# A hybrid encoder on one core: every second weight unit of the mixers is split by transfers instead of by VectorE or GpSimd

## The chip, the core and the metric

The kernel runs on one core of one Trainium2 chip. The metric is the device time of one execution in microseconds. TensorE multiplies; ScalarE (ACT), VectorE (DVE) and GpSimd (POOL) do the elementwise work; SyncE (SP) issues the transfers. Work on one engine runs in the order in which it was queued there; engines wait for each other by semaphores.

## The reference

Two layers (DEPTH = 2) over 256 tokens of 1024 features, all in float32. Each layer is a feed-forward half step, a mixer with four branches, and another feed-forward half step:

```python
for l in range(DEPTH):
    x = x + 0.5 * swiglu_ffn(x, ffn1_norm[l], ffn1_wi[l], ffn1_wo[l])
    h = rmsnorm(x, mix_norm[l])
    (a_q, a_k, a_v, sc_u, c_qlat, c_kvlat, c_krope, lru_u, gate_lin) = jnp.split(
        h @ w_in[l], split_idx, axis=-1)
    o_a = gqa_mixer(...)        # 8 query heads, 2 key/value heads, rotary
    o_b = shortconv_mixer(...)  # width-3 convolution, gated
    o_c = mla_mixer(...)        # low-rank attention, 8 heads
    o_d = rglru_mixer(...)      # width-4 convolution, gated recurrences both ways
    branches = jnp.stack([o_a, o_b, o_c, o_d], axis=2)
    y = jnp.einsum('bsnc,ncd->bsnd', branches, w_branch[l])
    g = jax.nn.sigmoid(gate_lin.reshape(b, s, N_BRANCH, d))
    x = x + jnp.sum(g * y, axis=2) @ w_out[l]
    x = x + 0.5 * swiglu_ffn(x, ffn2_norm[l], ffn2_wi[l], ffn2_wo[l])
```

A feed-forward half step has matrices of 1024 x 5632 and 2816 x 1024. The mixer's `w_in` is 1024 x 8096, `w_branch` 4 x 512 x 1024, `w_out` 1024 x 1024; the low-rank up-projections and the recurrence's gates are small.

## The kernel before

**Products in three parts.** Every float32 operand is kept as a high and a low part, both in the type float32r, that sum to it. A product is three matmuls (`mm`, lines 208 to 212): high by high, high by low, low by high. Each weight piece of 128 rows by 128 columns (some are 336, 384 or 512 columns wide) meets all 256 tokens.

**The stream of weights.** The class `Weights` (line 66) streams all weights once, in the order of their use. That order is found by a first pass over the program with `Null` objects. `chunks_of` (line 134) groups the pieces into units of at most 1024 columns (`UNIT`; the first two are smaller), and units into transfers of at most 2048 columns (`MAXC`), except the first seven (`FIRST`), which hold one unit each and go to buffers of their own. `load` (line 82) issues one transfer on SP into a tile of `raw_pool` (three buffers of 2048 columns). `split` (line 100) makes a unit's parts:

```python
a = self.nc.scalar.copy(hi[:, :w], src)
self.n += 1
eng = self.nc.gpsimd if self.share and self.n % self.share == 0 else self.nc.vector
b = eng.tensor_tensor(lo[:, :w], src, hi[:, :w].bitcast(F32), op=ALU.subtract)
```

So ScalarE casts the unit to `hi` (line 110) and VectorE or GpSimd subtracts it from the raw weights to give `lo` (line 113). There are four buffers each for `hi` and `lo`. `next` (line 121) hands out pieces and calls `split` so that two units (`AHEAD`) are called for ahead of the one in use. `share` decides who subtracts: 0 is VectorE alone; from the mixer's first slot until `gate(3, 0)` it is 4, every fourth unit on GpSimd; from the slot of head 15 until the output projection it is 1, all on GpSimd.

**The start.** Lines 233 to 242 issue on SP four transfers of `x`, ten transfers of weights (`EARLY`) and then the identity, the parameters and the tables, in that order. The identity is used first in `scale_rows` (line 358).

**A mixer.** It begins with token-major products of the latents and of queries, keys and values. Then comes a list of slots (line 905): each has an attention head or none, some products to keep TensorE fed (input projections, gates, branch up-projections), and other work. The grouped-query heads (0 to 7) run beside the short convolution and the recurrence, the low-rank heads (8 to 15) beside the gates. Of the other work GpSimd has: the rotary swaps (line 311), powers for the norms, the recurrence's products over 1024 columns (lines 709 to 711, 722, 723), a product of the gelu (667), squares (803, 808) and the gated sums (880). A head takes VectorE's row maximum (448), the exponential on ScalarE (454), a scaling of the probabilities on VectorE (462), transposes on TensorE (469), their split (217, 218) and the value products on TensorE (966).

**Order.** The program is written with tile pools; a planner orders the instructions on each engine by their place in the program, their dependencies and its own estimate of durations, and gives out buffers. Only the instructions marked `keep_in_program_order` (the constants' transfers and the opening work) keep their place.

Of the kernel before, what the change touches and what calls it, by code (L numbers as in the profile page):

```python
# [17 lines left out]
T = 256  # L18
# [10 lines left out]
# columns of the combined input projection  # L29
# [11 lines left out]
# per-layer columns of the packed per-channel parameters  # L41
# [7 lines left out]
# per-layer columns of the packed row vectors, then the rotary tables  # L49
# [7 lines left out]
# the first transfers of weights hold one unit each; so many of them go ahead of the constants  # L57
FIRST = 7
EARLY = 10
# GQA heads between a head's scores and its use  # L60
LAG = 2
# opening work in order: operand pair of x's tile k (k), split of the next weights (-1), square of tile k (10 + k)
START = (0, -1, 1, 2, 3, -1, 4, 5, -1, 6, 7, -1, 10, 11, 12, -1, 13, 14, 15, 16, 17)


class Weights:
    """Streams the weights in the order of their use and hands out each piece as two float32r
    parts that sum to it. Without the packed array it only records that order."""

    AHEAD = 2  # L70

    def __init__(self, nc, flat=None, order=None, raw_pool=None, hi_pool=None, lo_pool=None):
# [5 lines left out]
        self.spare = None  # where the first transfers go  # L78
        self.share, self.n = 0, 0  # every share-th low part on GpSimd
        self.ci, self.off, self.loaded, self.ready, self.now = 0, 0, [], [], []  # L80

    def load(self):
        if self.recording:
            return
        units = self.chunks[self.ci]
# [7 lines left out]
        self.off += P * cols  # L93
        self.ci += 1
        at = 0
        for u in units:
            self.loaded.append((u, raw, at))
            at += sum(p[4] for p in u)

    def split(self):  # L100
        if self.recording:
            return ()
        if not self.loaded:
            self.load()
        u, raw, at = self.loaded.pop(0)
        w = sum(p[4] for p in u)
        hi = self.hi_pool.tile([P, UNIT], F32R, tag="hi", name="hi")
        lo = self.lo_pool.tile([P, UNIT], F32R, tag="lo", name="lo")
        src = raw[:, at : at + w]
        a = self.nc.scalar.copy(hi[:, :w], src)  # L110
        self.n += 1
        eng = self.nc.gpsimd if self.share and self.n % self.share == 0 else self.nc.vector
        b = eng.tensor_tensor(lo[:, :w], src, hi[:, :w].bitcast(F32), op=ALU.subtract)  # L113
        out, o = [], 0
        for p in u:
            out.append((p, hi[:, o : o + p[4]], lo[:, o : o + p[4]]))
            o += p[4]
        self.ready.append(out)
        return a, b

    def next(self, *piece):
# [3 lines left out]
        if not self.now:  # L125
            while len(self.ready) <= self.AHEAD and (self.loaded or self.ci < len(self.chunks)):
                self.split()
            self.now = self.ready.pop(0)
# [5 lines left out]
def chunks_of(order):  # L134
    """Pieces grouped into split units of at most UNIT columns, those into transfers of MAXC."""
# [20 lines left out]
class Null:  # L156
    """Stands for every object of a trace that only records the order of the weights."""
# [18 lines left out]
def hybrid_encoder(ctx: ExitStack, tc: tile.TileContext, xT, par, rows, ident_d, flat, out, order=None):  # L176
# [31 lines left out]
    def mm(out, lhs, rhs, start, stop):  # L208
        """out (+)= lhs.T @ rhs, each operand a (high, low) pair of float32r."""
# [4 lines left out]
    def split(hi, lo, src, scale=None):  # L214
        """hi + lo = src (times a per-partition or constant scale)."""
# [931 lines left out]
```

## Time and profile before

| what | value |
|---|---|
| median of 3 runs (lowest to highest) | 1417.77 us (1417.46 to 1418.06) |
| profiled execution, span from first to last instruction | 1416.7 us |
| busy share: TensorE, VectorE, ScalarE, GpSimd | 97%, 71%, 53%, 17% |
| transfers | 240.81 MB, 170 GB/s on average |
| granted TensorE clock, mean | 0.990 |

The profiled execution's own time is shown as its span; the three runs have no profile. The four feed-forward half steps and the two mixers follow each other: the first mixer runs from about 200 to 505 us of the span, the second from about 900 to 1210 us. In the profile, L12 is line 12 of the kernel. A tile is shown by its program name (`hi<-raw`: reads raw, writes hi). "PEclk" is the clock that TensorE was granted, 1.00 being the full 2.4 GHz. A matmul's listed duration overlaps that of its neighbours, so the rate of matmuls is read from counts or from start times.

### The profile page before, as it was taken

Reading aid. Unit: us, or ns where it says so; the run is one execution under the profiler, and the core shown is the slowest. Engines: PE = TensorE matmul, PEld = TensorE weight load, DVE = VectorE, ACT = ScalarE, POOL = GpSimd, SP = SyncE. Lnnn points to the kernel's source line nnn. Section 1 sums busy time; section 2 is a strip of 40 time slices with the busy share of each in tenths; the row PEclk is TensorE's granted clock in tenths of the full one; section 3 lists DMA queues with packets and bytes.
Section 4 is the critical chain, followed back from the end, with each engine's and each line's share of the span. In section 5 each row is a group of like instructions: output and inputs, shape, how many; then the busy total and the mean of one; then the engine's idle time right before and its main releaser. Section 6 shows DMA issues by size and latency. Waiting matters only on the chain.

```text
span 1416.7 us, 26507 instructions
## 1 busy us (share of the span) xinstructions
PE 1377.8 (97%) x11184; PEld 1364.5 (96%) x11184; DVE 999.4 (71%) x1334; ACT 746.0 (53%) x1104; POOL 247.0 (17%) x199
## 2 busy tenths in 40 slices
PE   8999999997999999999999999999989999999999
PEld 8999999897899999999999999999889999999999
DVE  6666558989877676666566665599899777666653
ACT  6444447584556555444444444566745564554432
POOL 3200004329610400000000000032456104000000
PEclk9999999999999999999999999999999999999999
DMA  7555545433454355555555555444325534555552
GB/s 280 184 187 191 183 152 202 149 120 129 155 179 149 120 180 188 193 184 179 183 180 194 188 179 180 163 176 165 118 108 183 197 127 149 179 179 181 186 206 76
DMA packets 35831, 240.81 MB, mean 170 GB/s; under 512 B 3968, under 2 KB 5376, under 8 KB 9472
## 3 DMA queue, kind: packets, MB, share of 16 engines
q1 hardware_dynamic: 35712, 239.12, 47.6%
q8 instruction: 87, 1.43, 0.4%
q14 instruction: 32, 0.26, 0.1%
HBM read 238.06 MB, written 1.05 MB: 169 GB/s over the span
## 4 chain that ended last, share of the span: by engine, by line
PE 88%; DVE 5%; issue 2%; POOL 2%; ACT 1%; DMA 0%; SPq 0%; DVEq 0%; POOLq 0%; ACTq 0%
PE pg L211 6%; PE pu L211 6%; PE pg L212 6%; PE pg L210 6%; PE pu L212 6%; PE pu L210 6%; PE po L211 6%; PE po L210 6%; PE po L212 6%; PE pgt L210 4%; PE pgt L211 3%; PE pgt L212 3%; PE pa L211 2%; PE pa L212 2%; PE pa L210 2%
## 5 line engine op out<-in xcount | busy, mean ns | idle before, releaser
L110 ACT CAST hi<-raw 128x1024 fp32r<-128x1024 f32 (+4 forms) x459 | 474.2, 1035 | 500.5 <-PE po L211 117.0
L113 DVE TENSOR_TENSOR lo<-raw,hi 128x1024 fp32r<-128x1024 f32 (+4 forms) x428 | 539.5, 1261 | 276.1 <-ACT hi L110 274.5
L210 PE MATMUL pg<-xh,hi 128*128 128x256 f32 x704 | 199.0, 283 | 6.1 <-ACT hi L110 6.1
L211 PE MATMUL pg<-xl,hi 128*128 128x256 f32 x704 | 199.5, 283 | 0.0
L212 PE MATMUL pg<-xh,lo 128*128 128x256 f32 x704 | 199.2, 283 | 0.0
L211 PE MATMUL pu<-xl,hi 128*128 128x256 f32 x704 | 198.8, 282 | 0.0
L210 PE MATMUL pu<-xh,hi 128*128 128x256 f32 x704 | 198.4, 282 | 0.0
L212 PE MATMUL pu<-xh,lo 128*128 128x256 f32 x704 | 198.3, 282 | 0.0
L211 PE MATMUL po<-hl,hi 128*128 128x256 f32 x704 | 198.0, 281 | 0.0
L212 PE MATMUL po<-hh,lo 128*128 128x256 f32 x704 | 197.7, 281 | 0.0
L210 PE MATMUL po<-hh,hi 128*128 128x256 f32 x704 | 197.7, 281 | 0.0
L210 PE MATMUL pgt<-xnh,hi 128*128 128x256 f32 x512 | 146.4, 286 | 0.0
L212 PE MATMUL pgt<-xnh,lo 128*128 128x256 f32 x512 | 145.0, 283 | 0.7 <-DVE lo L113 0.7
L211 PE MATMUL pgt<-xnl,hi 128*128 128x256 f32 x512 | 145.5, 284 | 0.0
L210 PEld LDWEIGHTS pg<-xh,hi 128*128 128x128 f32 x704 | 133.8, 190 | 6.4 <-ACT hi L110 6.4
L212 PEld LDWEIGHTS pg<-xh,lo 128*128 128x128 f32 x704 | 133.8, 190 | 0.2 <-DVE lo L113 0.2
L211 PEld LDWEIGHTS pg<-xl,hi 128*128 128x128 f32 x704 | 133.8, 190 | 0.0
L212 PEld LDWEIGHTS pu<-xh,lo 128*128 128x128 f32 x704 | 133.1, 189 | 0.2 <-DVE lo L113 0.2
L211 PEld LDWEIGHTS pu<-xl,hi 128*128 128x128 f32 x704 | 133.2, 189 | 0.0
L210 PEld LDWEIGHTS pu<-xh,hi 128*128 128x128 f32 x704 | 133.0, 189 | 0.0
L211 PEld LDWEIGHTS po<-hl,hi 128*128 128x128 f32 x704 | 132.7, 188 | 0.0
L212 PEld LDWEIGHTS po<-hh,lo 128*128 128x128 f32 x704 | 132.6, 188 | 0.0
(301 smaller groups left out, 3052.7 us busy)
## 6 DMA issues: line engine op xcount, KB each, us to landing
raw<-weights SPq DMA_DIRECT2D x205, 1024.0 KB, 4.8
raw<-weights SPq DMA_DIRECT2D x9, 768.0 KB, 4.3
raw<-weights SPq DMA_DIRECT2D x4, 896.0 KB, 4.6
raw<-weights SPq DMA_DIRECT2D x3, 1008.0 KB, 4.7
raw<-weights SPq DMA_DIRECT2D x5, 512.0 KB, 8.0
out<-xg SPq DMA_DIRECT2D x8, 128.0 KB, 2.1
raw<-weights SPq DMA_DIRECT2D x1, 1016.0 KB, 4.8
raw<-weights SPq DMA_DIRECT2D x1, 968.0 KB, 4.6
```

What stands on the lines that cost most here:

```text
L110: a = self.nc.scalar.copy(hi[:, :w], src)
L113: b = eng.tensor_tensor(lo[:, :w], src, hi[:, :w].bitcast(F32), op=ALU.subtract)
L210: TE.matmul(out, lhs[0], rhs[0], start=start, stop=False)
L211: TE.matmul(out, lhs[0], rhs[1], start=False, stop=False)
L212: TE.matmul(out, lhs[1], rhs[0], start=False, stop=stop)
```

## The change

Units with an odd number whose pieces all belong to the mixers (`w_in`, `lru`, `qup`, `kvup`, `wb`, `wout`) are "queued". Such a unit is never loaded raw. GpSimd issues a transfer from the weights in memory to `hi`, which casts to float32r on its way; ScalarE writes the negative of `hi` into `lo`; GpSimd issues a second transfer of the same weights that adds to `lo`. All other units are split as before, always with VectorE; `share` is gone. `prepare` calls a queued unit up to four units ahead of the one in use (`LEAD`), others two ahead as before. `raw_pool` has two buffers instead of three, `hi_pool` and `lo_pool` five instead of four. A transfer holds one unit alone where it or its neighbour is queued. Comments are blanked too, which keeps the line numbers of unchanged places near their old ones.

```diff
+QUEUED = ("w_in", "lru", "qup", "kvup", "wb", "wout")
+
+def queued(i, unit):
+    return i % 2 == 1 and all(p[0] in QUEUED for p in unit)
...
     AHEAD = 2
+    LEAD = 4
...
     def load(self):
         if self.recording:
             return
+        while len(self.chunks[self.ci]) == 1 and queued(self.unit_of(self.ci), self.chunks[self.ci][0]):
+            self.skip()
...
+    def pair(self):
+        hi = self.hi_pool.tile([P, UNIT], F32R, tag="hi", name="hi")
+        lo = self.lo_pool.tile([P, UNIT], F32R, tag="lo", name="lo")
+        return hi, lo
...
         a = self.nc.scalar.copy(hi[:, :w], src)
-        self.n += 1
-        eng = self.nc.gpsimd if self.share and self.n % self.share == 0 else self.nc.vector
-        b = eng.tensor_tensor(lo[:, :w], src, hi[:, :w].bitcast(F32), op=ALU.subtract)
...
+        b = self.nc.vector.tensor_tensor(lo[:, :w], src, hi[:, :w].bitcast(F32), op=ALU.subtract)
         return a, b
+
+    def queue(self, n):
+        _, src, w, _ = self.units[n]
+        self.made[n] = hi, lo = self.pair()
+        self.nc.gpsimd.dma_start(hi[:, :w], src)
+        self.nc.scalar.activation(lo[:, :w], hi[:, :w].bitcast(F32), AF.Copy, scale=-1.0)
+        self.nc.gpsimd.dma_start(lo[:, :w], src, accum_op=ALU.add)
+
+    def prepare(self):
+        for n in range(self.taken, min(self.taken + self.LEAD + 1, len(self.units))):
+            if n in self.made:
+                continue
+            if self.units[n][3]:
+                self.queue(n)
+            elif n <= self.taken + self.AHEAD:
+                while n not in self.made:
+                    self.split()
...
-        if cur and (n + w > MAXC or i <= FIRST):
+        if cur and (n + w > MAXC or i <= FIRST or queued(i, u) or queued(i - 1, units[i - 1])):
...
-    raw_pool = ctx.enter_context(tc.tile_pool(name="raw_pool", bufs=3))
-    hi_pool = ctx.enter_context(tc.tile_pool(name="hi_pool", bufs=4))
-    lo_pool = ctx.enter_context(tc.tile_pool(name="lo_pool", bufs=4))
+    raw_pool = ctx.enter_context(tc.tile_pool(name="raw_pool", bufs=2))
+    hi_pool = ctx.enter_context(tc.tile_pool(name="hi_pool", bufs=5))
+    lo_pool = ctx.enter_context(tc.tile_pool(name="lo_pool", bufs=5))
...
-        def share(n):
-            return lambda: setattr(W, "share", n)
```

## Rows read from the trace of the kernel before

**Rows 1.** us from:to, length; busy us (count) of PE, PEld, DVE, ACT, POOL; PEclk, DMA share, GB/s.

```profile
200.00:240.00 40.00, 40.00 (x269) 40.00 (x268) 28.27 (x55) 27.11 (x53) 8.13 (x16) 1.00 0.56 195
240.00:300.00 60.00, 57.83 (x468) 55.58 (x466) 57.08 (x84) 36.49 (x64) 25.11 (x27) 1.00 0.40 142
300.00:362.00 62.00, 51.13 (x364) 48.65 (x364) 55.22 (x66) 37.24 (x64) 40.16 (x14) 0.92 0.36 127
...
400.00:480.00 80.00, 79.89 (x680) 79.68 (x679) 57.16 (x91) 48.18 (x89) 7.55 (x5) 1.00 0.41 146
480.00:505.00 25.00, 22.64 (x177) 22.23 (x176) 16.54 (x29) 10.21 (x18) 14.75 (x7) 0.93 0.46 163
...
940.00:1000.00 60.00, 59.44 (x483) 57.51 (x482) 57.02 (x87) 38.02 (x69) 20.78 (x16) 1.00 0.42 145
1000.00:1060.00 60.00, 51.13 (x371) 49.00 (x370) 51.40 (x66) 36.33 (x63) 31.65 (x13) 0.94 0.32 112
...
1180.00:1210.00 30.00, 27.01 (x203) 26.60 (x203) 22.16 (x35) 12.33 (x21) 14.94 (x7) 0.89 0.34 117
60.00:180.00 120.00, 120.00 (x1011) 120.00 (x1011) 74.16 (x86) 55.79 (x66) 0.00 (x0) 1.00 0.53 187
```

**Rows 2.** TensorE in order of time, 318 to 362 us: start, duration, instruction, wait.

```profile
328.51 0.58 PE L966 MATMUL pov<-pl,vg 128*128 128x256 f32 x1 [4.53 <-DVE pl L218]
...
329.54 0.41 PE L210 MATMUL pgt<-xnh,hi 128*128 128x256 f32 x1
329.75 0.41 PE L211 MATMUL pgt<-xnl,hi 128*128 128x256 f32 x1
```

**Rows 3.** VectorE's and GpSimd's groups, 240 to 380 us: busy us, mean ns | idle.

```profile
L113 DVE TENSOR_TENSOR lo<-raw,hi 128x1024 fp32r<-128x1024 f32 x26 | 35.2, 1354 | 8.6 <-ACT hi L110 8.4
L462 DVE TENSOR_SCALAR pe<-pe,sm 128x256 f32<-128x256 f32 x16 | 15.8, 1031 | 0.2
...
L113 DVE TENSOR_TENSOR lo<-raw,hi 128x768 fp32r<-128x768 f32 x3 | 6.0, 2009 | 0.0
...
L113 POOL TENSOR_TENSOR lo<-raw,hi 128x1024 fp32r<-128x1024 f32 x8 | 20.1, 2512 | 34.9 <-ACT hi L110 34.9
L113 POOL TENSOR_TENSOR lo<-raw,hi 128x768 fp32r<-128x768 f32 x1 | 6.6, 6557 | 0.0
```

**Rows 4.** VectorE in order of time: two pairs of the softmax scaling.

```profile
317.24 4.69 DVE L462 TENSOR_SCALAR pe<-pe,sm 128x256 f32<-128x256 f32 x2
...
476.56 0.62 DVE L462 TENSOR_SCALAR pe<-pe,sm 128x256 f32<-128x256 f32 x2
```

**Rows 5.** The weight split's groups: the page's casts, then 60 to 180 us.

```profile
L110 ACT CAST hi<-raw 128x1024 fp32r<-128x1024 f32 (+4 forms) x459 | 474.2, 1035 | 500.5 <-PE po L211 117.0
...
L113 DVE TENSOR_TENSOR lo<-raw,hi 128x1024 fp32r<-128x1024 f32 x43 | 52.5, 1222 | 29.2 <-ACT hi L110 29.2
L110 ACT CAST hi<-raw 128x1024 fp32r<-128x1024 f32 x42 | 44.0, 1048 | 60.2 <-PE po L211 20.3 <-PE pg L211 19.9 <-PE pu L211 17.8
```

**Rows 6.** Transfers by size: count, KB each, median us from issue to landing.

```profile
raw<-weights SPq DMA_DIRECT2D x205, 1024.0 KB, 4.8
...
raw<-weights SPq DMA_DIRECT2D x5, 512.0 KB, 8.0
...
raw<-weights SPq DMA_DIRECT2D x1, 744.0 KB, 4.2
...
ident<-ident SPq DMA_DIRECT2D x1, 64.0 KB, 13.9
```

**Rows 7.** The opening in order of time: SP's issues, TensorE's use of the identity.

```profile
10.13 0.33 SPq L242 DMA_DIRECT2D ident<-ident  x1
...
22.44 35.71 SPq L92 DMA_DIRECT2D raw<-weights  x7
...
26.73 0.61 PE L358 MATMUL pb<-ident,rt 128*128 128x128 f32 x4
```

**Rows 8.** GpSimd in order of time: two of the recurrence's products.

```profile
327.40 5.95 POOL L711 TENSOR_TENSOR thi<-thi,thr 128x1024 f32<-128x1024 f32 x2
```

More of the change, by code (lines that the diff above doesn't have):

```diff
@@ L78, in __init__ @@
         self.spare = None
-        self.share, self.n = 0, 0
         self.ci, self.off, self.loaded, self.ready, self.now = 0, 0, [], [], []
+        self.units, at = [], 0
+        for c in self.chunks:
+            cols = sum(p[4] for u in c for p in u)
+            o = 0
+            for u in c:
+                w = sum(p[4] for p in u)
+                src = flat[at : at + P * cols].rearrange("(p c) -> p c", p=P)[:, o : o + w]
+                self.units.append((u, src, w, queued(len(self.units), u)))
+                o += w
+            at += P * cols
+        self.made, self.taken = {}, 0
     def load(self):
@@ L92, in load, with unit_of, skip @@
         self.nc.sync.dma_start(raw[:, :cols], src)
-        self.off += P * cols
+        at, first = 0, self.unit_of(self.ci)
+        self.skip()
+        for i, u in enumerate(units):
+            self.loaded.append((first + i, raw, at))
+            at += sum(p[4] for p in u)
+    def unit_of(self, ci):
+        return sum(len(c) for c in self.chunks[:ci])
+    def skip(self):
+        self.off += P * sum(p[4] for u in self.chunks[self.ci] for p in u)
         self.ci += 1
[L95 to L98, printed above, removed]
+    def pair(self):
+        hi = self.hi_pool.tile([P, UNIT], F32R, tag="hi", name="hi")
+        lo = self.lo_pool.tile([P, UNIT], F32R, tag="lo", name="lo")
+        return hi, lo
     def split(self):
@@ L104, in split @@
             self.load()
[L105 to L108, printed above, removed]
+        n, raw, at = self.loaded.pop(0)
+        w = self.units[n][2]
+        self.made[n] = hi, lo = self.pair()
         src = raw[:, at : at + w]
         a = self.nc.scalar.copy(hi[:, :w], src)
-        self.n += 1
-        eng = self.nc.gpsimd if self.share and self.n % self.share == 0 else self.nc.vector
-        b = eng.tensor_tensor(lo[:, :w], src, hi[:, :w].bitcast(F32), op=ALU.subtract)
[L114 to L118, printed above, removed]
-        return a, b
+        b = self.nc.vector.tensor_tensor(lo[:, :w], src, hi[:, :w].bitcast(F32), op=ALU.subtract)
+        return a, b
+    def queue(self, n):
+        _, src, w, _ = self.units[n]
+        self.made[n] = hi, lo = self.pair()
+        self.nc.gpsimd.dma_start(hi[:, :w], src)
[10 more added lines that the diff above has]
+                    self.split()
     def next(self, *piece):
@@ L125, in next @@
         if not self.now:
-            while len(self.ready) <= self.AHEAD and (self.loaded or self.ci < len(self.chunks)):
-                self.split()
-            self.now = self.ready.pop(0)
+            self.prepare()
+            hi, lo = self.made.pop(self.taken)
+            o = 0
+            for p in self.units[self.taken][0]:
+                self.now.append((p, hi[:, o : o + p[4]], lo[:, o : o + p[4]]))
+                o += p[4]
+            self.taken += 1
         p, hi, lo = self.now.pop(0)
@@ L899, in call @@
             return lambda: f(*args)
-        def share(n):
-            return lambda: setattr(W, "share", n)
         slots = [
-            (None, [proj("pxb", C_XB, 0, lru_conv)], [share(4), lat_norms, gqa_norms, lat_scale]),
+            (None, [proj("pxb", C_XB, 0, lru_conv)], [lat_norms, gqa_norms, lat_scale]),
             (None, [proj("pxb", C_XB, 1, lru_conv)], [lat_transpose, call(gqa_rotate, 0), call(gqa_rotate, 1), call(lru_taps, 0)]),
@@ L920, in mixer @@
             (None, [gate(1, 3), up(1, 3, "ob"), call(mla_up, 1, "kvup")], [lru_out, call(mla_square, 0)]),
-            (None, [gate(3, 0), up(3, 0, "od")], [share(0), call(mla_sum, 0), call(mla_swap, 0), call(mla_square, 1)]),
+            (None, [gate(3, 0), up(3, 0, "od")], [call(mla_sum, 0), call(mla_swap, 0), call(mla_square, 1)]),
             (None, [gate(3, 1), up(3, 1, "od")], [call(mla_sum, 1), call(mla_query, 0), call(mla_swap, 1), mla_values]),
@@ L931, in mixer @@
             (14, [gate(2, 2)], []),
-            (15, [gate(2, 3), share(1)], []),
+            (15, [gate(2, 3)], []),
             (None, [up(0, 2, "oa"), up(0, 3, "oa")], []),
@@ L1011, in mixer @@
             split(*merged[n], m, scale=0.5)
-        W.share = 0
         pws = [bank("pw")[:, :T] for _ in range(2)]
```

## The prediction

> **What bounds the kernel now.** I read a table of stretches first, then TensorE in order of time inside the worst stretch, then VectorE's and GpSimd's groups there, and last the DMA rows. TensorE is listed as busy in all of 120 us of one stretch and in 51 of 62 of another [rows 1], but a busy TensorE is not TensorE at full rate, so I count matmuls. In the feed-forward stretch from 60 to 180 us there are 1011 in 120 us [rows 1]: 0.1187 us each. A weight unit of eight 128-column pieces is 24 matmuls, so it lasts 2.85 us there, and a pair of units 5.70 us. Everywhere else I ask what the counted matmuls would take at that price.
>
> In the mixers the answer is uneven. The stretch from 400 to 480 us has 680 matmuls, worth 80.7 us: nothing is lost. From 300 to 362 us there are 364, worth 43.2 of 62 us: 18.8 us lost. The same stage of the second layer, 1000 to 1060, has 371, worth 44.0: 16.0 lost. The stage ahead of it loses 4.5 us (240 to 300, 468 matmuls) and 2.7 us (940 to 1000, 483). The end of the mixers loses 4.0 us (480 to 505, 177) and 5.9 us (1180 to 1210, 203). That is 51.9 us in all [rows 1]. It is the most that any relief inside the mixers can return. Some matmuls there are wider than 256 columns, so the true loss is a little smaller.
>
> In those same stretches VectorE is nearly full: 57.1 of 60 us and 55.2 of 62 us, against 74 of 120 us in the feed-forward stretch [rows 1]. TensorE's order of time names it: at 328.51 us the value product has stood 4.53 us for the low part that VectorE makes, and the matmuls right after are spaced 0.21 us instead of 0.12 [rows 2]. The granted clock of the stretch is 0.92, so part of the loss is the clock falling to its lower level (1.2 GHz) after the idle stretch, and it comes back when the idle time does not occur [rows 1, 2].
>
> **Why VectorE is full there.** Between 240 and 380 us it subtracts 29 units and GpSimd nine [rows 3]. Beside running GpSimd work VectorE's operations stretch: the softmax scaling takes 1.03 us on average there, though it costs 0.31 us alone (a pair in 0.62) and a pair once took 4.69 [rows 3, 4]. GpSimd pays too: its 768-column subtraction took 6.6 us, the 1024-column ones 2.5 [rows 3].
>
> **The change, part by part.**
>
> *Removed from VectorE and GpSimd.* The weight copies count 459 [rows 5]; the four feed-forward halves need 4 x (44 + 22) = 264 units by their shapes, so the mixers have 195, and every second one, about 97, is now queued. From 240 to 380 us there are 38 units; VectorE keeps 19 of them instead of 29. Ten times 1.25 us, near its cost alone of 1.22 [rows 5], is 12.5 us less. The stretching also shrinks: the 16 scalings alone lose 16 x (1.03 - 0.31) = 11.5 us, and GpSimd's subtractions (20.1 + 6.6 us) are about a third of its 75 us of work there (25.1 us to 300, 40.2 to 362, and I put 10 for the rest) [rows 1, 3]. A third of 11.5 us is some 4 us, and other forms give a few more. So VectorE is relieved of at least 16 us in a stage that loses about 23.
>
> How much reaches TensorE? Nothing, if the remaining GpSimd products (recurrence and gelu, near 3 us each [rows 8]) hold the same chain; all, if VectorE were the only cause. I take half, because two thirds of GpSimd's work there stays. Half of 18.8 + 16.0 + 4.5 + 2.7 = 42.0 is 21 us. At the mixers' end GpSimd takes every low part now, and VectorE's sums stretch beside it; I take half again of 9.9, 5 us. Together 26 us, bounds 0 and 52.
>
> *ScalarE.* Each queued unit loses a cast of 1.05 us and gets a negation of the same shape on the same engine [rows 5]: zero. What changes is what it waits for: a transfer. Behind it on ScalarE stand the other casts and the evacuations, and TensorE waits for these through its banks. ScalarE is busy 37 of 62 us in the worst stretch [rows 1], so short waits are covered; without that cover each costs its length.
>
> *The two transfers.* No transfer from GpSimd is in this trace. The nearest rows: 1024 KB land 4.8 us after issue and 744 KB 4.2 us, so a straight line gives 3.7 us for the 512 KB of a unit; the opening's 512 KB transfers, queued behind others, took 8.0 [rows 6]. I take 3.7 for the cast, since the mixers' DMA share is 0.36 to 0.56 and not full [rows 1]. The adding transfer must also read its destination: 3.7 to 7.4 us, and I take 5. The time GpSimd spends on issuing one lies between 0.33 us, an issue on SP [rows 7], and 2.5 us, one of its 1024-column subtractions; I take 1, nearer the issue that it resembles. A queued unit is then ready after 3.7 + 1 + 1.05 + 1 + 5 = 11.8 us, waits excluded. Five buffers, taken in the order of the calls, let the cast start some five units before use: 14.2 us at full rate. So the slack is 2.4 us, and where GpSimd's own products stand in front (three near 3 us each in a row [rows 8]) it is gone. What is late next is the first matmul of that unit. I charge 5 us for each mixer, 10 in all: bounds 0 and, with the high prices, far more (rivals).
>
> *Bandwidth.* Each pair of units moves 1.5 MB where it moved 1. The share of 0.56 at 200 to 240 us becomes 0.84, or 1.12 if an adding transfer occupies the engines twice [rows 1]. I take the first: no cost. The second costs 12% of that stretch, 5 us a mixer.
>
> *Buffers.* Two raw buffers instead of three: in the feed-forward steady state SP issues one transfer for each pair that VectorE finishes, seven from 22.44 us on in 35.71 us [rows 7], one per 5.7 to 5.9 us, and it lands in 4.8 [rows 6]; the second buffer covers the meanwhile. Zero. The covered margin is under 1 us, and a fifth high and low buffer adds one more unit behind it.
>
> *The opening.* Ten transfers go ahead of the constants; seven have buffers of their own, so the tenth now waits for a raw buffer. Its release is the event that the eleventh waits for today, at 22.44 us, while the identity is issued at 10.13 and lands 13.9 us later, at 24.0 [rows 6, 7]. It would be issued near 22.9 and land behind 1 MB, near 27.5; TensorE first uses it at 26.73 [rows 7]. I charge 1 us, bounds 0 and 4 (VectorE's first use of the parameters can stand in front of two splits).
>
> *The sum.* 1416.7 (the span) - 26 + 10 + 1 = 1401.7. The median of the runs is 1417.77, 1.1 above the span, so 1402.8: I predict 1403 us, with 1390 to 1410 as this case's own range.
>
> By the Trainium skill (DMA: Bandwidth & Descriptors, Anatomy of one DMA, SWDGE path) a transfer issued from GpSimd costs about 2.0 us plus its bytes at 436 GB/s; for 512 KB that is an estimate of 3.2 us. With it for the cast the slack would be 0.5 us larger; no run here shows it yet.
>
> **The rivals.**
>
> *GpSimd's queue becomes the pace (slower).* GpSimd works in order. If the adding transfer of one unit stands ahead of the casting transfer of the next queued one, GpSimd holds still from the cast's issue until the negation is done: landing + negation + second issue. That cycle must fit in a pair's 5.70 us. Low prices give 3.7 + 1.05 + 0.33 = 5.1 and it fits; with my 1 us for the issue and a short wait on ScalarE it is 6.4, 0.7 too long. A mixer runs from about 200 to 505 us; without the 122 us of its two slow stretches 183 us are left, 32 pairs, 64 in both mixers; 64 x 0.7 = 45 us lost, of which half the gain, 13, is taken off: 1418 + 32 = 1450 us. It decides from a cycle of about 6.1 us on (64 x 0.4 = 26). For it: the numbers are at the edge, and in the recurrence GpSimd's products, 2.98 us each [rows 8], stand in front of the issues. Against it: the order on each engine is planned, not that of the calls, so other work may be put between, and GpSimd is busy only 7.6 of 80 us in the full-rate stage [rows 1]. With the opening's 8.0 us landing the cycle is 10.05 us and the loss 64 x 4.35 = 278 us; there nine transfers queue on full engines, which the mixers' share does not show, so that end stays outside the range.
>
> By the Trainium skill (SBUF — State Buffer, The "DVE blocks DMA" trap) GpSimd cannot write a transfer's descriptors while VectorE runs a fast copy or tensor-scalar operation; that speaks against the change. No run here shows it.
>
> As a mechanism of this kernel: if each softmax scaling of the stage held an issue for its full time, 15.8 us a mixer [rows 3], and half reached TensorE, the forecast would become 1403 + 16 = 1419, no change.
>
> *The gain is given back (no change).* The issue held up as just said, the DMA engines full at 200 to 240 us (10 us for both mixers), or GpSimd's remaining products keeping the chain: 1415 to 1420 us.
>
> *VectorE was the only cause (faster by more).* Three quarters of 51.9 us come back, 39, and the units arrive in time: 1380 us. For it: VectorE's busy time in the stage; against it: the products that stay on GpSimd.
>
> **How the numbers follow.** A measurement of this kernel tells about 0.2% (2.8 us) from no change. Forecast 0.42; larger gain 0.10; gain given back 0.10; GpSimd's queue 0.38, which spreads from 1425 to well above 1450. Faster 0.52, same 0.10, slower 0.38. The range leaves out half of the larger gain and about an eighth above: 1383 to 1465.
>
> **What would show it.** Right: in the two stages at 300 and 1000 us VectorE falls under 50 of 62 us and the matmul count per 62 us rises toward 400; nothing under GpSimd from the weight subtraction; negations of 1.05 us that wait little. Wrong: waits of TensorE for the adding transfer, ScalarE standing before the negation, and matmuls fewer than 680 in the 80 us that lose nothing today. The greatest risk is the landing time of the casting and adding transfers; the next is the tenth transfer of the opening.

## The result, and the profile after

The changed kernel takes 1486.8 us (median of 4 runs, 1483.62 to 1490.14) against 1417.91 us of the kernel before beside it (4 runs, 1417.46 to 1419.27): a ratio of 1.0481, 95% interval 1.0461 to 1.0501. It is slower by 4.8%; the forecast was 1403 us, the range 1383 to 1465. The profiled execution spans 1481.7 us.

Where the time went is read from the first product into `pa` and the last into `pw`, which enclose a mixer. (`pw` is the output projection, which the 505 and 1210 us named ahead leave out.) Of the first mixer of the changed kernel (view of one tile on TensorE: durations, first and last start, forms):

```profile
L261 PE MATMUL pa<-hi,xh x64: 312/334/522, 199.4 to 237.3; 128*128 128x336 f32 x32, 128*128 128x384 f32 x32
```

```profile
L263 PE MATMUL pw<-mgh,lo x64: 274/280/392, 525.5 to 554.3; 128*128 128x256 f32 x64
```

So it lasts 199.4 to 554.3, 354.9 us; read the same way it lasted 325.5 us before. The second lasts 360.9 against 322.5 us. Between and around them nothing is lost: the opening is 1.0 us longer, the two feed-forward halves between the mixers 2.5 shorter, the last one 1.3 shorter. 29.4 + 38.4 + 1.0 - 2.5 - 1.3 = 65.0 us, the difference of the spans.

The stretches of the changed kernel, columns as in [rows 1]:

```profile
200.00:240.00 40.00, 36.24 (x218) 35.44 (x218) 17.12 (x38) 23.55 (x48) 14.99 (x28) 0.96 0.89 230
240.00:300.00 60.00, 56.35 (x459) 54.51 (x457) 44.86 (x80) 38.03 (x69) 25.74 (x41) 1.00 0.88 229
300.00:362.00 62.00, 49.95 (x377) 47.60 (x376) 49.61 (x68) 35.22 (x60) 28.55 (x21) 0.93 0.61 151
400.00:480.00 80.00, 74.99 (x606) 74.24 (x606) 40.68 (x63) 39.50 (x64) 27.55 (x29) 0.96 0.89 228
...
1180.00:1240.00 60.00, 51.72 (x411) 51.17 (x409) 28.53 (x57) 31.87 (x63) 11.29 (x15) 0.94 0.70 172
```

VectorE did come free: 44.9 and 49.6 us where [rows 1] had 57.1 and 55.2. The stage that had lost most has 377 matmuls instead of 364. But the stretch that lost nothing, 400 to 480 us, has 606 instead of 680, and 200 to 240 us has 218 instead of 269. The DMA share there is 0.89 in place of 0.41 and 0.56. The feed-forward stretch, 60 to 180 us, is as before: 1012 matmuls against 1011.

The new work in the page's groups, and GpSimd's transfers by size (count, KB, median us from issue to landing; the landing is the arrival, and it is counted from the start of the issue):

```profile
L155 ACT ACTIVATE lo<-hi 128x1024 fp32r<-128x1024 f32 (+3 forms) x96 | 98.9, 1030 | 177.8 <-DMA hi<-weights 173.9
L154 POOL DMA_DIRECT2D hi<-weights x96 | 68.1, 709 | 448.2 <-DVE acc L389 167.9
L156 POOL DMA_DIRECT2D lo<-weights x96 | 85.0, 891 | 275.0 <-ACT lo L155 244.7
```

```profile
hi<-weights POOLq DMA_DIRECT2D x79, 512.0 KB, 6.4
lo<-weights POOLq DMA_DIRECT2D x79, 512.0 KB, 6.5
```

Negation and issues cost what was forecast (1.03 us; 0.7 and 0.9). The landings don't: 6.4 and 6.5 us. ScalarE stands 173.9 us before casting transfers, GpSimd 244.7 us before negations. TensorE meets the end of that chain as here (order of time):

```profile
404.83 0.47 PE L263 MATMUL pgt<-xnh,lo 128*128 128x256 f32 x1 [1.77 <-DMA lo<-weights]
405.10 0.42 PE L261 MATMUL pgt<-xnh,hi 128*128 128x256 f32 x1
405.32 0.42 PE L262 MATMUL pgt<-xnl,hi 128*128 128x256 f32 x1
```

It waits 1.77 us for an adding transfer, and the products behind it are spaced 0.21 us instead of 0.12 for 3.5 us: after the wait the clock is at its lower level (1.2 GHz; granted 0.91 over 400 to 420 us), so this wait costs nearly twice its length.

Added up over the run, TensorE's largest waits for adding transfers are these (us in total, times, longest):

```profile
PE pgt L263 <- DMA lo<-weights: 12.0, 4, 4.7
...
PE pa L262 <- DMA lo<-weights: 10.6, 6, 3.0
...
PE pup L263 <- DMA lo<-weights: 4.8, 4, 2.3
```

All of them come to 34.0 us, and those for casting transfers to 4.8; before there were none. In all TensorE stands idle for 81.6 us of the span instead of 38.9, and is listed as busy for 1400.1 us instead of 1377.8, with the granted clock at 0.980 instead of 0.990. So late parts of queued units make up nearly all of the new idle time; the other 22 us are slower work.

### The profile page after: what moved, and what is told of

Same layout as the page of the kernel before. It is cut to its first block, busy times and chain, and to the rows that moved or that the text cites. A ratio compares the mean times of both kernels' runs of the same rounds, so it can differ in the third digit from the quotient of the medians.

```text
span 1481.7 us, 26788 instructions
## 1 busy us (share of the span) xinstructions
PE 1400.1 (94%) x11184; PEld 1379.4 (93%) x11184; DVE 890.0 (60%) x1269; ACT 743.8 (50%) x1104; POOL 290.9 (20%) x360
## 4 chain that ended last, share of the span: by engine, by line
PE 55%; issue 20%; DMA 9%; POOL 7%; DVE 5%; ACT 2%; SPq 0%; POOLq 0%; DVEq 0%; ACTq 0%
DMA hi<-weights 6%; PE pu L262 6%; PE pu L261 5%; PE pu L263 5%; PE pg L262 5%; PE pg L263 5%; PE pg L261 5%; PE po L262 5%; PE po L261 5%; PE po L263 4%; DMA lo<-weights 3%; POOL lo L156 2%; POOL hi L154 2%; DVE lo L148 1%; DMA raw<-weights 1%
## 5 line engine op out<-in xcount | busy, mean ns | idle before, releaser
L148 DVE TENSOR_TENSOR lo<-raw,hi 128x1024 fp32r<-128x1024 f32 (+2 forms) x363 | 447.3, 1233 | 289.1 <-ACT hi L147 287.8
L147 ACT CAST hi<-raw 128x1024 fp32r<-128x1024 f32 (+2 forms) x363 | 375.5, 1036 | 406.7 <-PE po L262 117.4
L263 PE MATMUL pg<-xh,lo 128*128 128x256 f32 x704 | 199.4, 283 | 0.0
L155 ACT ACTIVATE lo<-hi 128x1024 fp32r<-128x1024 f32 (+3 forms) x96 | 98.9, 1030 | 177.8 <-DMA hi<-weights 173.9
L263 PE MATMUL pgt<-xnh,lo 128*128 128x256 f32 x512 | 150.7, 294 | 12.0 <-DMA lo<-weights 12.0
L154 POOL DMA_DIRECT2D hi<-weights x96 | 68.1, 709 | 448.2 <-DVE acc L389 167.9
L261 PE MATMUL pgt<-xnh,hi 128*128 128x256 f32 x512 | 151.3, 296 | 0.0
L262 PE MATMUL pgt<-xnl,hi 128*128 128x256 f32 x512 | 150.7, 295 | 0.0
L156 POOL DMA_DIRECT2D lo<-weights x96 | 85.0, 891 | 275.0 <-ACT lo L155 244.7
```

The source lines that it names most:

```text
L148: b = self.nc.vector.tensor_tensor(lo[:, :w], src, hi[:, :w].bitcast(F32), op=ALU.subtract)
L154: self.nc.gpsimd.dma_start(hi[:, :w], src)
L155: self.nc.scalar.activation(lo[:, :w], hi[:, :w].bitcast(F32), AF.Copy, scale=-1.0)
L156: self.nc.gpsimd.dma_start(lo[:, :w], src, accum_op=ALU.add)
L261: TE.matmul(out, lhs[0], rhs[0], start=start, stop=False)
L262: TE.matmul(out, lhs[0], rhs[1], start=False, stop=False)
```

## The experiments

Three theories, as they stand in the expectations: **F**: the DMA engines are full. **L**: a queued unit's transfers take longer than the buffers give it. **Q**: the order of waits (cast, negation, adding transfer) on GpSimd and ScalarE sets the pace. "Mixers" below are both mixers together, first to last product, from the profile: 648.0 us before, 715.8 in the changed kernel. A time without an interval is that of a single run.

### The change part by part

**e1_resident_raw**: the mixers' units that aren't queued take a scaled part of x for their raw weights, so 48 MB need not move.

```diff
+        if all(p[0] in QUEUED for u in units for p in u) and len(units) == 1:
+            self.loaded.append((self.unit_of(self.ci), self.kept, 0))
...
```

> The mixers' even units are not loaded: their splits read (scaled) a part of x that lies on chip, so SP moves nothing in the mixers, and GpSimd's transfers stay as they are. Theory F (the DMA engines are full: the two GpSimd transfers of a unit take 0.71 of the engines from 400 to 460 us and SP's another 0.23): the share in the mixers falls to about 0.7, a GpSimd transfer lands in 5 us or less instead of 6.5, and the time falls to 1400 to 1425 us. Theory L (a queued unit takes some 17 us whatever else moves, and five buffers give 14): landing stays at 6.4, time 1470 to 1487. Theory Q (GpSimd's queue holds still for the negation and sets the pace): time 1470 to 1487 too.

Measured: 1462.5 us, mixers 690.5; the share at 400 to 460 us falls from 0.94 to 0.64, the landings only to 5.9 and 5.6 us. A third of the loss comes back with a third of the engines' load. The time lies between the two expectations: F alone doesn't hold, and neither do L and Q as put there, under which nothing was to come back.

**e2_second_plain**: the second transfer overwrites `lo` instead of adding to it.

```diff
-        self.nc.gpsimd.dma_start(lo[:, :w], src, accum_op=ALU.add)
+        self.nc.gpsimd.dma_start(lo[:, :w], src)
```

> The second transfer no longer adds but overwrites the low part (casting, as the first does), with the same order and waits; the low part is thus wrong. If reading the destination for the sum is what fills the engines (theory F, adding kind): the DMA share of GpSimd's queue over the span falls from 29% to 22% or less and the time to 1430 to 1455 us. If a casting transfer costs as much as an adding one, or under theories L and Q: 1480 to 1490 us, share unchanged.

Measured: 1419.61 us, mixers 651.4, landings 5.0 and 4.7 us. The same bytes on the same queues without the addition: nearly all the loss is gone, more than F had forecast, and against L and Q, which had been put as if the landings would not change. TensorE waits 10.2 us for queued transfers instead of 38.8.

**e3_every_fourth**: `i % 4 == 1` in `queued`.

> Every fourth unit of the mixers is queued instead of every second. Theory F: the engines' share at full rate is about 0.35 + 0.33 = 0.7, not full, so transfers land in 5 us, VectorE keeps three quarters of the subtractions, and the time is 1400 to 1420 us, perhaps under the kernel before. Theory L: each of the 48 queued units still comes late by the same few us: about half of the loss stays, 1445 to 1455 us. Theory Q: the cycle of 7 us fits easily in 11.4 us: 1400 to 1420.

Measured: 1429.7 us, ratio 1.0077 [1.006, 1.0094], mixers 657.2. Half as many queued units, a seventh of the loss: less than L had forecast, but more time than F and Q allowed, so it decides nothing.

**e4_no_adding**: the adding transfer is left out; the low part stays the negated high part.

> The adding transfer is left out, so the low part is only the negative of the high part. All theories: faster than the changed kernel. Theory F: share at full rate 0.35 + 0.23 = 0.6, time 1390 to 1410 us. Theory L: a queued unit is ready after some 8 us, inside its lead: 1390 to 1410. Theory Q: GpSimd never waits for a negation: 1390 to 1410. It tells what the relief of VectorE and of GpSimd's subtractions is worth when the low parts are never late: my forecast put it at 26 us, 1392.

Measured: 1407.01 us, mixers 635.4, although ScalarE still waits 75.5 us for casts, which land in 4.2 us. So this is what the relief of VectorE and GpSimd is worth when the low parts don't come late: some 12 us (the kernel before ran at 1418.73 beside it), not 26.

**e11_half_adding**: the adding transfer covers half the columns, so half of each low part is the negated high part.

```diff
+        self.nc.gpsimd.dma_start(lo[:, : w // 2], src[:, : w // 2], accum_op=ALU.add)
```

> The changed kernel, but the adding transfer covers only the first half of a unit's columns; the other half of the low part stays the negated high part, so a part of the computation is changed. Engines' time for a pair of units falls from 5.1 to 3.8 us by the prices of e7_transfers_alone, and the adding transfer lands sooner. Without it e4_no_adding took 1407, whole it takes 1487. Theory F: once the engines have room, most comes back: 1410 to 1430 us. Theory Q (the queue's order and waits): about half, 1445 to 1460.

Measured: 1438.06 us, mixers 666.9, landings 5.4 and 4.8. Between the two expectations; alone it decides nothing.

### The transfers by themselves

**e7_transfers_alone** and **e9_mix_alone** replace the computation by transfers.

> Computes nothing of the reference. It only issues transfers of 512 KB, ten at a time and then four one after the other, with nothing beside them: plain ones from SP, plain ones from GpSimd, casting ones from GpSimd, adding ones from GpSimd; then ten casting ones beside a VectorE that runs scalings without a pause. Theory F: an adding transfer occupies the engines about twice as long as a casting one (from the shares of the other runs about 0.38 against 0.23 % of the span for each MB, so some 2.6 against 1.6 us of all 16 engines for 512 KB when they queue); alone it lands in 4.5 to 6 us, a casting one in 3.5 to 4.5. Theory L: both occupy the engines alike, and an adding one only lands later. Beside VectorE's scalings the issues on GpSimd take under 1.5 us each if the mixers' 0.6 to 0.9 us hold, far more if VectorE's fast operations hold up the writing of descriptors.

VectorE reads each landed tile, so its starts are the landings. The first two lines are from the stretch of ten casts, the next two from that of ten adding ones, then one of each alone, then the nine casts issued beside VectorE's scalings:

```profile
57.18 0.15 DVE L254 COPY got<-c 128x1 f32<-128x1 f32 x1 [1.13 <-DMA c<-weights]
58.46 0.15 DVE L254 COPY got<-c 128x1 f32<-128x1 f32 x1 [1.12 <-DMA c<-weights]
...
83.61 0.15 DVE L254 COPY got<-c 128x1 f32<-128x1 f32 x1 [2.33 <-DMA c<-weights]
86.10 0.15 DVE L254 COPY got<-c 128x1 f32<-128x1 f32 x1 [2.33 <-DMA c<-weights]
...
131.51 0.53 POOL L269 DMA_DIRECT2D c<-weights  x1 [3.96 <-DVE c L257]
...
135.12 0.15 DVE L254 COPY got<-c 128x1 f32<-128x1 f32 x1 [2.75 <-DMA c<-weights]
...
149.46 0.88 POOL L272 DMA_DIRECT2D c<-weights  x1 [3.86 <-DVE c L257]
...
154.72 0.15 DVE L254 COPY got<-c 128x1 f32<-128x1 f32 x1 [4.41 <-DMA c<-weights]
...
174.68 6.67 POOL L269 DMA_DIRECT2D c<-weights  x9 [5.37 <-DVE c L257]
```

Queued behind each other, 512 KB take 1.28 us when cast and 2.5 us when added; alone they land 3.6 and 5.3 us after issue. An adding transfer occupies the engines twice as long, as F had it. By the Trainium skill (DMA: Bandwidth & Descriptors, Anatomy of one DMA, SWDGE path) the estimate was 3.2 us for 512 KB from GpSimd; the cast alone agrees roughly with 3.6. Beside VectorE's scalings an issue takes 6.67 / 9 = 0.74 us instead of 0.53, and the issues run in step with the scalings, one each:

```profile
176.90 0.69 DVE L286 TENSOR_SCALAR ev<-ew 128x1024 f32<-128x1024 f32 x1
176.97 0.73 POOL L269 DMA_DIRECT2D c<-weights  x1
```

The issue begins during the scaling and ends at 177.70 us, 0.1 us after it. The Trainium skill (SBUF — State Buffer, The "DVE blocks DMA" trap) warns that GpSimd cannot write a transfer's descriptors while VectorE runs such an operation; the trace agrees. With scalings of 0.69 us it costs 0.2 us an issue. In the changed kernel the casting issues are listed at 0.71 us in the mean, so the hold-up, which the forecast had priced at 16 us as part of a rival, has little room there.

> Computes nothing of the reference. It issues, with nothing else running, ten sets of 512 KB transfers at once: first sets of a plain and a casting one, then of a plain and two casting ones, then of a plain, a casting and an adding one (what a pair of units needs in the changed kernel), then of a casting and an adding one (what is left in e1_resident_raw). From the single kinds in e7_transfers_alone (1.28 us each for plain and casting, 2.5 us for adding) a set should take 2.6, 3.8, 5.1 and 3.8 us. Theory F needs the third set near the 6.4 us that a pair of units takes in 400 to 460 us of the changed kernel, so 6 us or more; if it is 5.1, the engines alone don't set that pace.

Ten sets of plain, cast and add run from the first issue at 81.2 to the last landing at 138.9 us: 5.8 us a set. The second kind takes 4.1, the last 4.2. The first landing, 4.1 us after its issue, is counted in, so 5.8 is an upper bound. It is below the 6.7 us between casts at 400 to 460 us of the changed kernel (nine in 60 us), but not far, and between the 5.1 and the 6 us of the expectation: it doesn't settle F.

### Order and lead

**e5_small_transfers** (`MAXC = 1024`, four raw buffers) is the control of **e6_six_high** (`LEAD = 5`, six high buffers, three raw).

> The changed kernel with raw buffers of 1024 columns, four of them, instead of two of 2048; high and low buffers stay five. It is the control of the run with six high buffers. Only the feed-forward transfers become smaller (512 KB instead of 1 MB). Theory L (a queued unit takes longer than the five buffers' lead): the mixers don't change, 1475 to 1500 us. Theory F (the DMA engines are the pace in the mixers): the same. In 400 to 460 us about 440 to 470 matmuls.

> The control with six high buffers and LEAD 5: a queued unit's casting transfer is called for one unit, 2.85 us, earlier, and raw buffers are three of 1024 columns. Theory L: a queued unit takes some 16 to 17 us against a lead of 14.2; 2.85 us more lead cover it, as the 3 us shorter transfers of e2_second_plain did, so 40 us or more of the 69 come back: 1420 to 1450 us, with over 490 matmuls in 400 to 460 us. Theory F: the engines move the same bytes by the same transfers, so nothing comes back: 1475 to 1490 us, under 470 matmuls, landings grow instead. Theory Q (GpSimd's order, one negation waited for before the next cast): no change either, 1475 to 1490, as the cycle on GpSimd stays.

Measured: 1497.05 and 1494.24 us, mixers 720.0 and 716.7. One more buffer, and with it one unit more of lead, returns nothing: L as I had put it falls.

**e10_resident_six**: e1 and e6 together.

> Two edits of before together: the mixers' other units aren't loaded (as in e1_resident_raw, so a part of the computation is changed and the engines have room), and six high buffers with LEAD 5 and raw buffers of 1024 columns (as in e6_six_high). Alone they gave 1462.5 and 1494 us. Theory L with F (the buffers' lead is too short, but the sixth buffer can't help while the engines are full): now it helps, 1420 to 1440 us. Theory Q (the order of waits on GpSimd and ScalarE is the pace): nothing more comes back, 1455 to 1475 us.

Measured: 1448.44 us, mixers 672.0, 18.5 less than e1. With room on the engines the buffer helps a little; it separates nothing.

**e13_deep** (cast called six units ahead, the rest four ahead, seven high buffers) and **e14_deep_resident** (the same with e1's edit):

```diff
+    LEAD = 6
+    FINISH = 4
...
+                if n not in self.cast:
+                    self.queue(n)
+                if n <= self.taken + self.FINISH:
+                    self.finish(n)
```

> The changed kernel with a longer and looser chain for a queued unit: its casting transfer is called for six units ahead instead of four, the negation and the adding transfer only when the unit is four ahead; seven high buffers instead of five, and raw buffers of 1024 columns, two of them (which may cost the feed-forward halves some us; the mixers are read by themselves). In GpSimd's order a casting transfer then always stands ahead of the adding one of the unit before, while the changed kernel has stretches in which cast and adding alternate in lockstep. Mixers from their first to their last product: 355 and 361 us in the changed kernel. Theory Q (GpSimd waits for each negation): both fall by 15 us or more. Theory F (engines): no fall, since the transfers are the same; 350 to 365 us each.

> The same with the mixers' other units not loaded (as in e1_resident_raw, a part of the computation is changed), so that the engines have room. Mixers: 347 and 344 us in e1_resident_raw. Theory L and Q: with room on the engines the longer and looser chain covers the transfers, and the mixers come to 315 to 325 us each, as without the adding transfer (316 and 320). Theory F alone, with landings of 6 us even at a share of 0.64: they stay above 335.

Measured: 1474.22 and 1449.12 us, mixers 654.4 and 635.2; the two small raw buffers cost the feed-forward halves (ScalarE waits 418.6 us for raw weights in e13). Stretches of e13, columns as in [rows 1]:

```profile
240.00:300.00 60.00, 54.80 (x415) 53.09 (x414) 44.50 (x79) 37.21 (x63) 25.77 (x43) 0.97 0.94 251
...
400.00:460.00 60.00, 60.00 (x512) 60.00 (x511) 33.27 (x48) 30.69 (x47) 26.51 (x29) 1.00 1.00 265
```

512 matmuls in 60 us is the full rate, at a share of 1.00 and landings of 8.7 and 7.2 us there. All bytes are still moved, and 61 of the 68 us are back. So F falls as the whole cause: full engines and long landings are compatible with the full rate if the chain is called early and loosely enough. They aren't so everywhere: from 240 to 300 us, at a share of 0.94, e13 makes only 415 matmuls (the changed kernel 459), and e14, with the other units' transfers gone, 469. Whether the engines' load or the two small raw buffers hold e13 back there isn't separated.

**e16_six_late_finish**: e6 with `FINISH = 3`, same buffers and transfers; only the call of negation and adding transfer comes later.

> e6_six_high with one edit: the negation and the adding transfer of a unit are called when it is three units ahead of use, its casting transfer five ahead as there. Buffers and transfers are the same; on GpSimd a casting transfer now always stands ahead of the adding one of the unit before, where e6 has many places in which the adding transfer stands alone between two casts. Mixers in e6: 364 and 353 us. Theory Q (the order on GpSimd): 325 to 340 us each. Theory L (lead): the adding transfer is called later than there, so no gain or a loss, 350 to 370.

Measured: 1436.02 us, mixers 660.1: 56.6 less than e6, 1% slower than before. First GpSimd in order of time in the changed kernel, then in e16, each at the end of the second mixer:

```profile
1190.59 0.85 POOL L154 DMA_DIRECT2D hi<-weights  x1
1199.97 0.84 POOL L156 DMA_DIRECT2D lo<-weights  x1 [8.53 <-ACT lo L155]
1201.78 0.56 POOL L154 DMA_DIRECT2D hi<-weights  x1 [0.96 <-PE pgt L263]
1209.81 0.85 POOL L156 DMA_DIRECT2D lo<-weights  x1 [7.48 <-ACT lo L155]
1210.36 0.86 POOL L154 DMA_DIRECT2D hi<-weights  x1
```

```profile
1176.13 0.55 POOL L155 DMA_DIRECT2D hi<-weights  x1 [5.24 <-PE pgt L274]
1177.34 0.87 POOL L164 DMA_DIRECT2D lo<-weights  x1 [0.67 <-ACT lo L163]
1183.44 0.55 POOL L155 DMA_DIRECT2D hi<-weights  x1 [5.23 <-PE pgt L274]
1184.98 0.87 POOL L164 DMA_DIRECT2D lo<-weights  x1 [0.99 <-ACT lo L163]
1190.76 0.55 POOL L155 DMA_DIRECT2D hi<-weights  x1 [4.91 <-PE pgt L274]
```

In the changed kernel each adding transfer waits 7 to 9 us for the negation of the cast issued just ahead of it, and the next cast comes behind it: 9.9 us a queued unit in these lines, at a share of only 0.70 and 411 matmuls in 60 us. In e16 the cast waits for a buffer that TensorE frees, the adding transfer hardly at all, and a queued unit takes 7.3 us in these lines; from 1140 to 1200 us it has

```profile
1140.00:1200.00 60.00, 60.00 (x512) 60.00 (x511) 33.98 (x68) 38.67 (x73) 15.34 (x20) 1.00 0.92 222
```

the full rate at a share of 0.92. Here the order of the calls set the pace, with room on the engines.

The order by itself isn't enough, though. In e2 GpSimd has all its work in the same order as the changed kernel; these are the same five issues there:

```profile
1140.87 0.53 POOL L154 DMA_DIRECT2D hi<-weights  x1 [1.78 <-PE pgt L263]
1147.32 0.53 POOL L156 DMA_DIRECT2D lo<-weights  x1 [5.92 <-ACT lo L155]
1149.08 0.53 POOL L154 DMA_DIRECT2D hi<-weights  x1 [1.23 <-PE pgt L263]
1156.22 0.53 POOL L156 DMA_DIRECT2D lo<-weights  x1 [6.61 <-ACT lo L155]
1156.74 0.54 POOL L154 DMA_DIRECT2D hi<-weights  x1
```

The same lockstep with landings of 5 us takes 7.9 us a queued unit, and TensorE is near its full rate (501 matmuls from 1100 to 1160 us). So the loss needs both, the slow adding transfer and the order; taking away either returns most of it. Nor does e16 tell GpSimd's standing from ScalarE's, since ScalarE's before casting transfers falls too, from 154.9 us in e6 to 39.7.

**e17_deep_at_once**: e13 with `FINISH = 6`.

> e13_deep with the negation and the adding transfer called together with the casting one, six units ahead: the lead stays, only the call is no longer put off. On GpSimd nearly all casts still stand ahead of the adding transfer of the unit before, since the buffers allow it. Mixers in e13: 331 and 323 us. If the order on GpSimd and the lead are what counts, and not the put-off call: 320 to 340 each; if the put-off call by itself (ScalarE not standing before the negation) did it: 345 to 365.

Measured: 1492.34 us, mixers 667.4, so 332 and 336 us, with the put-off call gone; the rest is the feed-forward halves' (ScalarE waits 492.6 us for raw weights). With deep buffers nearly every cast again stands ahead of the adding transfer of the unit before, so they loosen the order without the later call.

**e18_gpsimd_negates**: GpSimd writes the negation, in `queue`.

```diff
+        self.nc.gpsimd.tensor_scalar(lo[:, :w], hi[:, :w].bitcast(F32), -1.0, None, op0=ALU.mult)
```

> The changed kernel, but GpSimd writes the negated high part instead of ScalarE, so ScalarE never stands before a casting transfer; GpSimd itself does, and its negation of 1024 columns takes longer (its weight subtraction took 2.5 us). Over the runs so far the mixers' loss goes with ScalarE's wait for casting transfers (174 us, 68 lost; 98 us, 3; 40 us, 12) and not with GpSimd's wait for negations (245 us, 68; 217 us in e13_deep, 6). If ScalarE's standing is what costs: mixers 325 to 340 us each, against 355 and 361, though VectorE pays for GpSimd's work. If GpSimd's standing is what costs: 350 us or more each.

Measured: 1595.25 us, mixers 418 and 406 us. In the page's groups of this run:

```profile
L155 POOL TENSOR_SCALAR lo<-hi 128x1024 fp32r<-128x1024 f32 (+3 forms) x96 | 274.8, 2884 | 196.4 <-DMA hi<-weights 141.8
```

GpSimd now stands 141.8 us for casts and negates for 2.9 us each. With ScalarE out of the chain the loss grows, so ScalarE's standing isn't needed for a loss. But this run also lengthens each negation and puts GpSimd's work beside VectorE, so what ScalarE's standing adds in the changed kernel is not separated.

### What the relief was worth, and the buffers

**e8_no_gpsimd_subtraction**: the kernel before, `share(n)` always sets 0. **e15_vector_buffers**: the same with 2, 5 and 5 buffers. **e12_stage_only**: the changed kernel with every fourth unit queued, only from the first slot to `gate(3, 0)`.

> The kernel before with one part of the change alone: GpSimd subtracts no weights, VectorE subtracts them all; no transfer changes, buffers as before. It tells which half of the relief is worth something. If GpSimd's subtractions beside VectorE are what makes VectorE slow, 1395 to 1412 us; if VectorE's own load is the limit, nine or ten more units of 1.22 us in the stage of 240 to 380 us and the mixers' ends make it 1420 to 1440; my own guess is 1415 to 1430.

> e8_no_gpsimd_subtraction (1406.4 us) with the changed kernel's buffers: two raw buffers instead of three, five high and low ones instead of four. It prices the change of buffers alone, which my forecast took as zero: 1404 to 1409 us. In e12_stage_only ScalarE waited 78 us for raw transfers; if that is the two raw buffers' doing, it is 1412 to 1420 here.

> Only every fourth unit, and only of the stage from the first slot of a mixer to gate(3, 0), is split by the two transfers; VectorE subtracts all others and GpSimd none. It asks whether the transfers pay where VectorE is full and the DMA engines are not, beyond e8_no_gpsimd_subtraction (1406.4). If VectorE's load is a limit there: 1392 to 1403 us. If only GpSimd's subtractions were: 1404 to 1412. If one queued unit among three others is still late (theory L): 1412 to 1425.

| run | median us | ratio to before, 95% | mixers |
|---|---|---|---|
| e8 | 1406.4 | 0.9922 [0.9905, 0.9938] | 635.0 |
| e15 | 1408.45 | 0.9932 [0.9915, 0.9948] | 636.1 |
| e12 | 1417.22 | 0.9992 [0.9983, 1.0002] | 643.6 |

e8, with no transfer changed, beats both kernels; my own guess for it, 1415 to 1430, missed. Its stretches, and VectorE's groups from 240 to 380 us:

```profile
240.00:300.00 60.00, 60.00 (x487) 58.05 (x487) 56.00 (x95) 39.54 (x71) 14.28 (x22) 1.00 0.43 148
300.00:362.00 62.00, 56.68 (x413) 54.23 (x412) 56.69 (x68) 40.95 (x68) 33.23 (x15) 0.94 0.36 126
```

```profile
L113 DVE TENSOR_TENSOR lo<-raw,hi 128x1024 fp32r<-128x1024 f32 x36 | 51.0, 1422 | 5.7 <-ACT hi L110 5.7
L462 DVE TENSOR_SCALAR pe<-pe,sm 128x256 f32<-128x256 f32 x16 | 9.0, 604 | 0.2
```

VectorE makes 36 subtractions of 1024 columns instead of 26 [rows 3] and is as busy as before (56.0 and 56.7 us against 57.1 and 55.2, [rows 1]), yet TensorE makes 487 and 413 matmuls instead of 468 and 364, and 196 instead of 177 at the mixer's end. The scaling takes 0.60 us instead of 1.03 [rows 3]. In the second mixer the same stage (1000 to 1060 us) stays at 370 matmuls, and in e15 the first mixer's stage (300 to 362 us) stays at 362, though its mixers are as short as e8's: the count of one stretch depends on what falls into it, and the gain is read from the mixers. e15 is the same within the intervals: the buffers cost nothing measurable. e12 queues a few units where VectorE is full and is 8.8 us slower than e15, its like with VectorE alone, as L had it: the transfers don't pay there either.

## Why the prediction was wrong

**The step that failed is "The two transfers".** It charged 10 us for both mixers; they grew by 67.8 us, and some 12 us of relief (e4) lie against that, so the transfers cost some 80. Two things in it were off. The landings, taken as 3.7 and 5 us, are 6.4 and 6.5. With the negation the chain is 6.4 + 1.03 + 6.5 = 13.9 us, where the same terms of the forecast gave 9.8. (Its 11.8 us also counts two issues of 1 us, which lie inside the landings.) And the sum was made "waits excluded", though the waits decide: at the same buffers and transfers, e16 takes 56.6 us off e6 by calling negation and adding transfer later. Holding the chain against a lead isn't what decides, since e6 has one unit more of it and gains nothing. The cause behind the long landings is that an adding transfer occupies the engines twice as long as a casting one (e7) and, replaced by a plain one, lets both land in 5 us (e2).

**"GpSimd's queue becomes the pace" was the rival that came nearest**, with 0.38 and 1450 us, 37 short of the time. The mechanism it describes is in the lines under e16: GpSimd holds still from a cast's issue until the negation is done, 7 to 9 us, and with the order loosened (e16, e17) most of the loss goes. Its price was made of two wrong terms. The cycle, 6.4 us from a landing of 3.7, is 9.9 us in those lines. And it need not fit in 5.70 us: that is a pair of units in the feed-forward stretch, while in the mixers attention's matmuls stand between. From 400 to 480 us of the kernel before, at the full rate, ScalarE casts 23 units in 80 us, 7.0 us a pair:

```profile
L110 ACT CAST hi<-raw 128x1024 fp32r<-128x1024 f32 x23 | 24.1, 1048 | 15.8 <-PE pgt L211 9.0 <-PE pup L211 3.9 <-issue 1.1
```

What spoke against the rival, that the planner may put other work between, held in part of the mixers: at the end of the second, in those lines, cast and adding transfer alternate.

**"Bandwidth", no cost**: half wrong. The engines do come near full (0.89 at 200 to 240 us; 0.84 and 1.12 were the two ends). A full share is compatible with the full rate (e13 from 400 to 460 us), but landings are longer with it: 5.9 us for casts in e1, 6.4 in the changed kernel, 7.4 in e13.

**"ScalarE", zero**: a negation costs what a cast does, as said, but ScalarE stands 173.9 us in front of it. By e18 that isn't needed for a loss; its own part is open.

**"Removed from VectorE and GpSimd"**: the busy time fell as forecast, under 50 of 62 us. Its value, taken as 26 us, is some 12 (e4, e8), and its reason was wrong: VectorE's number of subtractions isn't what bound the stage, since e8 raises it and gains as much as e4. What counted was that GpSimd subtracts at all. Why is not shown: VectorE's scaling stretches beside it, as the forecast said, but a low part also takes 2.5 us and more on GpSimd [rows 3], and VectorE's own subtractions got no shorter without it (1.42 us against 1.35).

**"The opening"** (1 us) and **"Buffers"** (zero) were right: the identity is issued at 22.63 us, TensorE waits 0.55 us for it at 27.62, and the first mixer begins 1.0 us later.

## What to carry to other kernels

When work moves from an engine into a chain of transfers, write down what stands in order on the issuing engine: a step that waits for the landing of the transfer issued just ahead of it turns landing time into a cycle. Here the mixers lost 3 us by it with landings of 5 us (e2) and 68 us with landings of 6.4, so price the landing with the engines as full as the change makes them. Call the second half of such a chain later than the first, and check in the trace that the issuing engine waits for free buffers and not for its own chain. Before replacing work shared between two engines, try the kernel with one of them simply doing all of it.

## What the runs showed of the hardware

A transfer that adds to its destination moves 512 KB in 2.5 us of back-to-back time against 1.28 us for a casting or plain one (e7). Its issue is listed at 0.88 against 0.53 us when nothing else runs, and at up to 2.0 us with several outstanding (e9); but there issues follow each other every 0.55 us or so, so the listed time is not the time for which GpSimd is held. An issue that meets a VectorE scaling ends 0.1 us after it (e7). The DMA share reads 1.02 in a stretch of adding transfers alone, and one of 1.00 went with the full rate of TensorE in e13.
